# Mean over 8192 columns: the tail of the stream summed by VectorE alone, in seven pieces instead of five

## The chip, the cores and the metric

The kernel runs on one core of a Trainium2 chip. The metric is the device time of one execution, in microseconds (us), as the median of several runs. Six engines and queues appear in the text by their short names: DVE is VectorE, ACT is ScalarE, POOL is GpSimd, SP is SyncE, which here only issues DMAs, and the DMA queue behind SP is served by 16 DMA engines.

## What is computed

```python
x: (64, 256, 8192) float32
out = np.mean(x, axis=2)      # (64, 256)
```

That is 16384 rows of 8192 numbers, 536.87 MB to read, and one mean for each row, 64 KB to write.

## The kernel before

**Layout.** The 16384 rows are spread over 128 partitions, so a partition owns 128 rows. The rows are cut into three zones of 95, 17 and 16 rows a partition; within a zone a partition's rows lie one behind the other in memory. A load takes a pair of rows for each partition: 128 partitions by 16384 columns, 8 MB. Three buffers `buf0` to `buf2` take the pairs in turn.

**SP** issues every DMA, in program order. The first pair comes in three loads (lines 108, 109, 112), the next two at line 114, then a loop of 15 rounds with three loads each (line 121), then 15 loads written out (line 127). Each waits until DVE has freed its buffer (`free_sems`). The last pair of rows goes into `buf0`, called `tail` from there on, and it is cut into five pieces (line 133): SP waits once, for `buf0` to be free, and issues all five. The first four pieces land in `tail`, the last in the first columns of a small tile `fin`. Each piece has a semaphore of its own (`chunk_sems`). Behind them SP waits for POOL (`pool_sem`, line 134) and stores the scaled results of the first two zones (line 136, two stores), then it waits for `late_sem` and stores those of the last zone, `ends` (line 140). Nothing on SP can pass what stands ahead of it.

**DVE** sums a pair with one `tensor_reduce` (line 168 in the loop, line 178 for the first two of the last three pairs). For the last full pair and for the tail it uses the helper `halves` (line 151): one instruction adds the first half of a row to the second half element by element and also sums the result into one number, so that n columns take n / 2 steps. The instruction comes with a second one that reads the accumulator (DVE_READ_ACCUMULATOR2_ANT in the profile).

**The tail before.** `U` is 32 columns. The cuts are at columns 0, 9120, 13600, 15136, 15872 and 16384, so the pieces have 9120, 4480, 1536, 736 and 512 columns. Columns 0 to 8191 are the pair's first row; DVE sums it (4096 column halves) once the first piece is there. The second row is shared: of every one of the first four pieces ACT takes the first `mine[c]` columns (928, 1600, 544 and 256, line 207, with a running sum into one number), DVE the rest of the pieces 1 to 3 (2880, 992 and 480 columns, that is halves of 1440, 496 and 240). Each such sum is put into one of the eight columns `part(n)` behind the last piece in `fin`; seven are used, and POOL has zeroed the eighth (line 88) to keep the number even. When the last piece, all four ACT sums (`part_a`) and the DVE sums and POOL's zero (`part_d`) are there, `halves(fin, ...)` sums the 512 columns and the eight partial sums together (260 column halves), scales by 1 / 8192 and writes the last column of `ends`.

**POOL** scales all other results by 1 / 8192 in four instructions (line 97) after DVE's sum of the pair's first row (`owned_sem` at 4): 94, 2 and 16 columns into `scaled`, 15 into `ends`. When all four are done, SP may go on to the stores.

Of the kernel before, what the change touches and what calls it, by code (L numbers as in the profile page):

```python
# [5 lines left out]
F32 = mybir.dt.float32  # L6
ADD = mybir.AluOpType.add
X = mybir.AxisListType.X
COPY = mybir.ActivationFunctionType.Copy


def bass_global_avg_pool_1d_kernel(
# [6 lines left out]
    B, C, L = x.shape  # L19
# [20 lines left out]


    U = L // 256
    cuts = [0, L + 29 * U, L + 169 * U, L + 217 * U, L + 240 * U, 2 * L]
    mine = [29 * U, 50 * U, 17 * U, 8 * U]
    LAST = cuts[5] - cuts[4]
    NPART = 8

    flat = x.rearrange("b c l -> (b c) l")
    out_flat = out.rearrange("b c -> (b c)")
# [9 lines left out]
    with ExitStack() as ctx:  # L59
        sb = lambda n, s: ctx.enter_context(nc.sbuf_tensor(n, s, F32))  # L60
        sem = lambda n: ctx.enter_context(nc.semaphore(n))
        res = sb("res", [P, OWN - 1])
        scaled = sb("scaled", [P, EARLY])
        ends = sb("ends", [P, LATE])
        fin = sb("fin", [P, LAST + NPART])
        sb("pad", [P, (-nc.sbuf_base % ALIGN) // 4])
# [3 lines left out]
        free_sems = [sem(f"free_sem{i}") for i in range(NBUF)]  # L70
        first_sem = sem("first_sem")
        mixed_sem = sem("mixed_sem")
        chunk_sems = [sem(f"chunk_sem{c}") for c in range(5)]
        owned_sem = sem("owned_sem")
        part_d = sem("part_d")
        part_a = sem("part_a")
        pool_sem = sem("pool_sem")
        late_sem = sem("late_sem")
        out_sem = sem("out_sem")
# [2 lines left out]
        tail = bufs[0]  # L82
        part = lambda n: fin[:, LAST + n : LAST + n + 1]

        eng = nc.gpsimd
        eng.memset(part(NPART - 1), 0.0).then_inc(part_d, 1)  # L88
        eng.wait_ge(free_sems[0], LOADS0 + 1)
# [12 lines left out]
        eng = nc.sync  # L102
        def rows_of(n, k):
            z = 2 if n >= FROM[2] else 1 if n >= FROM[1] else 0
            return zone[z][:, (n - FROM[z]) * L : (n - FROM[z] + k) * L]

        a, z = rows_of(ZONE[0] - 1, 1), rows_of(ZONE[0], 1)
# [19 lines left out]
            eng.dma_start(bufs[b][:], rows_of(first_row(g), 2)).then_inc(in_sems[b], 16)  # L127
        eng.wait_ge(free_sems[0], LOADS0 + 1)
        two = rows_of(2 * NB, 2)
        for c in range(5):  # L130
            a, z = cuts[c], cuts[c + 1]
            dst = tail[:, a:z] if c < 4 else fin[:, 0:LAST]
            eng.dma_start(dst, two[:, a:z]).then_inc(chunk_sems[c], 16)  # L133
        eng.wait_ge(pool_sem, 4)
        for z in range(2):
# [11 lines left out]
        eng = nc.vector  # L147

        def halves(ap, to, done, scale=1.0):
            n = ap.shape[1] // 2  # L150
            eng.tensor_tensor_reduce(  # L151
                ap[:, 0:n],
                ap[:, 0:n],
                ap[:, n : 2 * n],
                scale=scale,
                scalar=0.0,
                op0=ADD,
                op1=ADD,
                accum_out=to,
            ).then_inc(done, 1)  # L160
# [29 lines left out]
                    )  # L190
        eng.wait_ge(chunk_sems[0], 16)
        halves(tail[:, 0:L], res[:, 2 * NB : 2 * NB + 1], owned_sem)
        for c in range(1, 4):
            eng.wait_ge(chunk_sems[c], 16)
            halves(tail[:, cuts[c] + mine[c] : cuts[c + 1]], part(3 + c), part_d)
        eng.wait_ge(chunk_sems[4], 16)
        eng.wait_ge(part_a, 4)
        eng.wait_ge(part_d, 4)
        halves(fin, ends[:, LATE - 1 : LATE], late_sem, inv)


        eng = nc.scalar
        for c in range(4):
            eng.wait_ge(chunk_sems[c], 16)
            a = cuts[c] if c else L
            ap = tail[:, a : a + mine[c]]
            eng.activation(ap, ap, COPY, accum_out=part(c)).then_inc(part_a, 1)  # L207


# [26 lines left out]
```

## Time and profile before

| | us |
|---|---|
| median of 3 runs | 1243.16 (1243.15 to 1243.31) |
| the profiled execution | 1243.06 |
| its span, first to last instruction | 1241.7 |
| HBM read 536.87 MB over the span | 432 GB/s |
| ACT: its four sums in the tail | 3.6 busy |
| POOL: its four scalings | 2.4 and 0.3 busy |

The profile comes from one execution. An "idle" time in brackets stands ahead of the instruction that it delayed, with what ended it. "SPq" is SP's queue, and its time is that of issuing DMAs, not of their transfers; the time of a transfer runs from its issue to its landing, so it includes the wait behind earlier transfers of the queue. In the row of a group, the numbers behind the first bar are the total busy time in us and the mean of one instruction in ns. A DVE group called CUSTOM_DVE_ANT_0 at line 151 is the helper `halves`; its column count is half of the columns that it sums. Among the landing times of the tail's five loads, the medians from issue are 32.2, 37.1, 38.5, 39.0 and 39.2 us: they stand behind the pair before them.

### The profile page before, as it was taken

What the parts mean: (1) busy time and instruction counts of PE and PEld (TensorE: products, weight loads), DVE (VectorE), ACT (ScalarE), POOL (GpSimd) and SP (SyncE); (2) the same over time, 40 slices, a digit from 0 to 9 for tenths busy, and PEclk for the clock granted to TensorE, in tenths of its full rate; (3) what the DMA queues carried; (4) which work ended last, traced back from release to release, by engine and by line L of the source; (5) the groups of instructions that cost most, each with busy time, mean ns of one, the idle gap of its engine ahead of it and who ended that gap; (6) DMA issues with size and microseconds to landing.
All of it is one profiled execution on the core that took longest, in us unless ns stands there. A gap on an engine that the chain in (4) does not pass through costs nothing. (4 is left out here: it accounts for less than half of the span.)

```text
span 1241.7 us, 549 instructions
## 1 busy us (share of the span) xinstructions
DVE 1084.1 (87%) x76; ACT 5.2 (0%) x9; POOL 2.9 (0%) x9
## 2 busy tenths in 40 slices
DVE  2898988989889898898898988989889898898987
ACT  0000000000000000000000000000000000000001
POOL 0000000000000000000000000000000000000000
DMA  9999999999999999999999999999999999999998
GB/s 405 439 439 439 439 435 410 439 439 439 439 439 433 412 439 439 439 439 439 426 418 439 439 439 439 439 422 422 439 439 439 439 439 422 422 439 439 439 439 374
DMA packets 10512, 536.94 MB, mean 432 GB/s; under 512 B 1552, under 2 KB 1552, under 8 KB 1936
## 3 DMA queue, kind: packets, MB, share of 16 engines
q1 hardware_dynamic: 10512, 536.94, 99.9%
HBM read 536.87 MB, written 0.07 MB: 432 GB/s over the span
## 5 line engine op out<-in xcount | busy, mean ns | idle before, releaser
L168 DVE TENSOR_REDUCE res<-buf 128x16384 f32 x60 | 1033.2, 17220 | 146.5 <-DVEq L167 146.5
L178 DVE TENSOR_REDUCE res<-buf 128x2 f32<-128x16384 f32 x2 | 34.4, 17220 | 4.0 <-DMA buf<-in_x_dram 4.0
L151 DVE CUSTOM_DVE_ANT_0 buf<-buf 128x4096 f32<-128x4096 f32 (+3 forms) x6 | 16.0, 2672 | 5.4 <-DMA buf<-in_x_dram 5.4
L207 ACT ACTIVATE buf<-buf 128x928 f32<-128x928 f32 (+3 forms) x4 | 3.6, 897 | 1233.7 <-DMA buf<-in_x_dram 1233.7
L97 POOL TENSOR_SCALAR scaled<-res 128x94 f32<-128x94 f32 (+2 forms) x3 | 2.4, 784 | 1235.0 <-DVE res L151 1234.8
L207 ACT ACT_TABLE_LOAD x1 | 1.3, 1283 | 0.7 <-PEq L221 0.7
L207 ACT ACTIVATION_READ_ACCUMULATOR buf<-buf 128x1 f32 x4 | 0.7, 187 | 0.0
L151 DVE CUSTOM_DVE_ANT_0 fin<-fin 128x260 f32<-128x260 f32 x1 | 0.4, 429 | 0.3 <-DMA fin<-in_x_dram 0.3
L97 POOL TENSOR_SCALAR ends<-res 128x15 f32<-128x15 f32 x1 | 0.3, 264 | 0.1
L151 DVE DVE_READ_ACCUMULATOR2_ANT res<- 128x1 f32 x3 | 0.3, 84 | 0.0
L151 DVE DVE_READ_ACCUMULATOR2_ANT fin<- 128x1 f32 x3 | 0.2, 81 | 0.0
L221 POOL MEMSET const-bfloat16-1.0<- 128x1 bf16 x1 | 0.1, 102 | 0.0
L221 POOL MEMSET const-uint8-127<- 128x1 uint8 x1 | 0.1, 102 | 0.0
L88 POOL MEMSET fin<- 128x1 f32 x1 | 0.1, 99 | 0.3 <-POOLq L221 0.3
L221 POOL MEMSET const-float32-0.0<- 128x1 f32 x1 | 0.1, 99 | 0.2 <-issue 0.2
L221 POOL MEMSET const-float32-1.0<- 128x1 f32 x1 | 0.1, 99 | 0.0
L151 DVE DVE_READ_ACCUMULATOR2_ANT ends<- 128x1 f32 x1 | 0.1, 82 | 0.0
## 6 DMA issues: line engine op xcount, KB each, us to landing
buf<-in_x_dram SPq DMA_DIRECT2D x1, 4560.0 KB, 32.2
buf<-in_x_dram SPq DMA_DIRECT2D x1, 4096.0 KB, 20.6
buf<-in_x_dram SPq DMA_DIRECT2D x1, 3072.0 KB, 11.4
buf<-in_x_dram SPq DMA_DIRECT2D x1, 2240.0 KB, 37.1
buf<-in_x_dram SPq DMA_DIRECT2D x1, 1024.0 KB, 4.6
buf<-in_x_dram SPq DMA_DIRECT2D x62, 40.3
buf<-in_x_dram SPq DMA_DIRECT2D x1, 768.0 KB, 38.5
buf<-in_x_dram SPq DMA_DIRECT2D x1, 368.0 KB, 39.0
```

Source lines behind the costliest of these rows:

```text
L88: eng.memset(part(NPART - 1), 0.0).then_inc(part_d, 1)
L97: eng.tensor_scalar(dst, src, inv, None, op0=mybir.AluOpType.mult).then_inc(pool_sem, 1)
L151: eng.tensor_tensor_reduce(ap[:, 0:n], ap[:, 0:n], ap[:, n : 2 * n], scale=scale, scalar=0.0, op0=ADD, op1=ADD, accum_out=to,).then_inc(do ...
L168: eng.tensor_reduce(sums[:, bass.ds(i, 1), b, :], bufs[b][:].rearrange("p (j l) -> p j l", j=2), X, ADD,).then_inc(free_sems[b], 1)
L178: eng.tensor_reduce(res[:, 2 * g : 2 * g + 2], bufs[b][:].rearrange("p (j l) -> p j l", j=2), X, ADD,).then_inc(free_sems[0] if b == 0 els ...
L207: eng.activation(ap, ap, COPY, accum_out=part(c)).then_inc(part_a, 1)
L221: nc = _bacc.Bacc("TRN2", target_bir_lowering=False, num_devices=1)
```

## The change

The tail is cut at columns 0, 8192, 9984, 12928, 14432, 15296, 15872 and 16384: seven pieces of 8192, 1792, 2944, 1504, 864, 576 and 512 columns. The first piece is now exactly the pair's first row. DVE sums every piece of the second row whole, as halves of 896, 1472, 752, 432 and 288 columns, into five partial sums; POOL's zero is the sixth, and the last sum takes 512 + 6 columns (259 column halves). The ACT program, its semaphore and its wait are gone. The last piece is the same 512 columns as before. In the changed kernel all lines from 11 on move up by one, and those behind the tail's loop by some more.

```diff
-COPY = mybir.ActivationFunctionType.Copy
...
     U = L // 256
-    cuts = [0, L + 29 * U, L + 169 * U, L + 217 * U, L + 240 * U, 2 * L]
-    mine = [29 * U, 50 * U, 17 * U, 8 * U]
-    LAST = cuts[5] - cuts[4]
-    NPART = 8
+    cuts = [0, L] + [L + n * U for n in (56, 148, 195, 222, 240)] + [2 * L]
+    PIECES = len(cuts) - 1
+    LAST = cuts[-1] - cuts[-2]
+    NPART = PIECES - 1
+    assert NPART % 2 == 0
...
-        chunk_sems = [sem(f"chunk_sem{c}") for c in range(5)]
+        chunk_sems = [sem(f"chunk_sem{c}") for c in range(PIECES)]
...
-        part_a = sem("part_a")
...
-        for c in range(5):
+        for c in range(PIECES):
             a, z = cuts[c], cuts[c + 1]
-            dst = tail[:, a:z] if c < 4 else fin[:, 0:LAST]
+            dst = tail[:, a:z] if c < PIECES - 1 else fin[:, 0:LAST]
...
-        for c in range(1, 4):
+        for c in range(1, PIECES - 1):
             eng.wait_ge(chunk_sems[c], 16)
-            halves(tail[:, cuts[c] + mine[c] : cuts[c + 1]], part(3 + c), part_d)
-        eng.wait_ge(chunk_sems[4], 16)
-        eng.wait_ge(part_a, 4)
-        eng.wait_ge(part_d, 4)
+            halves(tail[:, cuts[c] : cuts[c + 1]], part(c - 1), part_d)
+        eng.wait_ge(chunk_sems[PIECES - 1], 16)
+        eng.wait_ge(part_d, NPART)
         halves(fin, ends[:, LATE - 1 : LATE], late_sem, inv)
-
-
-        eng = nc.scalar
-        for c in range(4):
-            eng.wait_ge(chunk_sems[c], 16)
-            a = cuts[c] if c else L
-            ap = tail[:, a : a + mine[c]]
-            eng.activation(ap, ap, COPY, accum_out=part(c)).then_inc(part_a, 1)
```

## The prediction

> **What bounds the kernel now.** I read the page first, for which resource is full; then the chain that ended last; then the order of time of the last 60 us, because the diff touches nothing before it; then the shapes of the groups; then the loads and stores of the last stage.
>
> ```profile
> span 1241.7 us, 549 instructions
> DVE 1084.1 (87%) x76; ACT 5.2 (0%) x9; POOL 2.9 (0%) x9
> DMA  9999999999999999999999999999999999999998
> q1 hardware_dynamic: 10512, 536.94, 99.9%
> DMA 6%; DVE 3%; SPq 0%; issue 0%; DVEq 0%
> ```
>
> The one queue is full in every slice but the last: 536.94 MB take 99.9% of the time of sixteen engines, while VectorE (DVE) is busy for 87%. The kernel is a stream of loads, and everything else is wanted only to keep up. So a change in the tail can matter in two ways: by making the stream's last byte land at another time, or by making what follows that byte longer. The chain, in order of time, says the same of the end:
>
> ```profile
> 1200.62 39.18 DMA fin<-in_x_dram
> 1239.80 0.02 issue
> 1239.83 0.43 DVE fin L151
> 1240.26 0.01 DVE ends L151
> ```
>
> The last piece, issued at 1200.62, lands at 1239.80; VectorE starts on it 0.03 us later, works 0.43 us, and what is left up to 1241.7 is the store of the result. No ScalarE (ACT) instruction and no GpSimd (POOL) instruction is in this chain. The tail itself, in order of time:
>
> ```profile
> 1200.96 17.22 DVE L178 TENSOR_REDUCE res<-buf 128x2 f32<-128x16384 f32 x1 [2.16 <-DMA buf<-in_x_dram]
> 1220.27 4.42 DVE L151 CUSTOM_DVE_ANT_0 buf<-buf 128x4096 f32<-128x4096 f32 x1 [2.09 <-DMA buf<-in_x_dram]
> 1224.62 4.42 DVE L151 CUSTOM_DVE_ANT_0 buf<-buf 128x4096 f32<-128x4096 f32 x1
> 1228.96 0.08 DVE L151 DVE_READ_ACCUMULATOR2_ANT res<- 128x1 f32 x1
> 1231.01 4.43 DVE L151 CUSTOM_DVE_ANT_0 buf<-buf 128x4096 f32<-128x4096 f32 x1 [1.97 <-DMA buf<-in_x_dram]
> 1235.36 0.08 DVE L151 DVE_READ_ACCUMULATOR2_ANT res<- 128x1 f32 x1
> 1235.62 2.51 POOL L97 TENSOR_SCALAR scaled<-res 128x94 f32<-128x94 f32 x3 [1234.80 <-DVE res L151]
> 1236.35 1.66 DVE L151 CUSTOM_DVE_ANT_0 buf<-buf 128x1440 f32<-128x1440 f32 x1 [0.91 <-DMA buf<-in_x_dram]
> 1238.21 0.26 POOL L97 TENSOR_SCALAR ends<-res 128x15 f32<-128x15 f32 x1
> 1238.24 0.69 DVE L151 CUSTOM_DVE_ANT_0 buf<-buf 128x496 f32<-128x496 f32 x1 [0.22 <-DMA buf<-in_x_dram]
> 1238.50 0.82 SPq L136 DMA_DIRECT2D out_dram<-scaled  x2
> 1239.14 0.41 DVE L151 CUSTOM_DVE_ANT_0 buf<-buf 128x240 f32<-128x240 f32 x1 [0.20 <-DMA buf<-in_x_dram]
> 1239.47 0.19 ACT L207 ACTIVATION_READ_ACCUMULATOR buf<-buf 128x1 f32 x1
> 1239.48 0.08 DVE L151 DVE_READ_ACCUMULATOR2_ANT fin<- 128x1 f32 x1
> 1239.83 0.43 DVE L151 CUSTOM_DVE_ANT_0 fin<-fin 128x260 f32<-128x260 f32 x1 [0.26 <-DMA fin<-in_x_dram]
> 1240.29 0.33 SPq L140 DMA_DIRECT2D out_dram<-ends  x1
> ```
>
> The brackets carry the argument: ahead of every piece VectorE sat idle until a DMA landed, 1.97, 0.91, 0.22, 0.20 and 0.26 us. Its starts are therefore the landing times of the pieces (plus some 0.02 us each, which cancels in differences). ACT's last result is done at 1239.47 + 0.19 = 1239.66, that is 0.14 us before the last piece lands, so dropping ACT uncovers nothing by itself.
>
> **The change part by part.**
>
> *The two added loads.* The last pair still is 16384 columns in the same queue, and its last piece still is the same 512 columns; seven loads bring them where five did. From the starts above: 9120 columns took 1231.01 - 1220.27 = 10.74 us, or 1.1776 ns a column (the pair ahead took 19.31 for 16384, 1.179). At 1.1776 the smaller pieces should take 5.28, 1.81, 0.87 and 0.60; they took 5.34, 1.89, 0.90 and 0.69. So a piece costs 0.06, 0.08, 0.03 and 0.09 us beyond its bytes, 0.066 in the mean. Two more pieces: **+0.13 us**, with 0.06 and 0.18 as ends from the cheapest and the dearest of the four. The least is nothing; a gain is excluded, as the bytes and the queue stay the same. The upper end, far off, is a whole landing per load; that is a rival below. I take 0.13, for the added pieces (576 to 2944 columns) are of the sizes of those rows.
>
> *Where the pieces land.* With 1.1776 ns a column and 0.066 us a piece after the first, counted from 1220.27: 8192 columns at 1229.92, 1792 at 1232.09, 2944 at 1235.63, 1504 at 1237.46, 864 at 1238.55, 576 at 1239.29, 512 at 1239.96 (before: 1239.83).
>
> *What VectorE now does alone.* These groups give its price by columns:
>
> ```profile
> L151 DVE CUSTOM_DVE_ANT_0 buf<-buf 128x4096 f32<-128x4096 f32 x3 | 13.2, 4424 | 4.1 <-DMA buf<-in_x_dram 4.1
> L151 DVE CUSTOM_DVE_ANT_0 buf<-buf 128x1440 f32<-128x1440 f32 x1 | 1.7, 1659 | 0.9 <-DMA buf<-in_x_dram 0.9
> L151 DVE CUSTOM_DVE_ANT_0 buf<-buf 128x240 f32<-128x240 f32 x1 | 0.4, 409 | 0.2 <-DMA buf<-in_x_dram 0.2
> L151 DVE CUSTOM_DVE_ANT_0 fin<-fin 128x260 f32<-128x260 f32 x1 | 0.4, 429 | 0.3 <-DMA fin<-in_x_dram 0.3
> L97 POOL TENSOR_SCALAR scaled<-res 128x16 f32<-128x16 f32 x1 | 1.7, 1672 | 0.1
> L97 POOL TENSOR_SCALAR ends<-res 128x15 f32<-128x15 f32 x1 | 0.3, 264 | 0.1
> ```
>
> From 1440 to 4096 columns a half costs (4424 - 1659) / 2656 = 1.041 ns a column, and 1659 - 1440 x 1.041 = 160 ns stands fixed (240 columns by it: 410, measured 409). The halves of the new pieces are 4096, 896, 1472, 752, 432, 288 and, at the end, 259 columns: 4.42, 1.09, 1.69, 0.94, 0.61, 0.46 and 0.43 us. Back to back, the next starts 4.35 after a 4.42 (1220.27 to 1224.62). So: 4096 from 1229.92; 896 from 1234.27 to 1235.36, late by 2.18 but with nothing behind it yet; 1472 at its landing, 1235.63 to 1237.32; 752 from 1237.46 to 1238.40; 432 from 1238.55 to 1239.16; 288 from 1239.29 to 1239.75; the last at its landing, 1239.96. VectorE takes over 2.03 us (4.79 for the five middle pieces against 1.66 + 0.69 + 0.41 = 2.76) and hides them in its waits: ahead of the last five pieces it is still idle 0.27, 0.14, 0.15, 0.13 and 0.21. Cost on the path: **0**. If that cover were gone, what comes late is the 288 column piece, and only what exceeds 0.21 us reaches the end. The last half is one column shorter: 1 ns.
>
> *ScalarE leaves.*
>
> ```profile
> 0.72 1.28 ACT L207 ACT_TABLE_LOAD   x1 [0.72 <-PEq L221]
> 0.73 0.39 SPq L108 DMA_DIRECT2D buf<-in_x_dram  x1
> 1198.83 1.75 SPq L133 DMA_DIRECT2D buf<-in_x_dram  x4
> ```
>
> Its 5.2 us are off the chain, and the last sum's wait for it was over at 1239.66; 0. With it goes a table load of 1.28 us at the start, at 0.72, while SyncE's first load issues at 0.73 without waiting for it; 0.
>
> *GpSimd and SyncE.* The first row of the pair (8192 columns now, 9120 before) is done at 1234.34, not 1235.44, so GpSimd's scaling starts some 1.1 us earlier (0.18 after: 1234.52). SyncE issues the two stores of `scaled` when GpSimd is through, and the store of `ends` stands behind them in its order. GpSimd is sensitive to VectorE here: the 16 column scaling took 1672 ns beside the 264 of the 15 column one, and it ended at 1235.62 + 2.51 = 1238.13, just 0.12 after the 1440 column sum beside it ended (1236.35 + 1.66 = 1238.01). Now VectorE is never idle for long, so I let each of the four scalings get through in one gap: after 1235.36, 1237.32, 1238.40 and 1239.16, the last at 1239.28. The stores are issued 0.03 later, 1239.31 to 1240.13, and `ends` is wanted at 1239.96 + 0.46 = 1240.42. Margin 0.29; **0** on the path.
>
> The two added issues on SyncE go out with the others, 0.44 us each (1.75 / 4), so all seven from 1198.83 to 1201.9, the last 38 us before it lands: 0. Should the stores be issued early and cut in between the loads, they would cost little. In these stretches (busy columns, clock, share of the DMA engines, GB/s) the loads' landing at 1239.80 is followed by the two stores' packets, 0.44 of 0.2 us:
>
> ```profile
> 1239.60:1239.80 0.20, 0.00 (x0) 0.05 (x1) 0.00 (x0) 1.00 0.07 8
> 1239.80:1240.00 0.20, 0.17 (x1) 0.00 (x0) 0.00 (x0) 1.00 0.44 42
> out_dram<-scaled SPq DMA_DIRECT2D x1, 47.5 KB, 1.6
> out_dram<-ends SPq DMA_DIRECT2D x1, 8.0 KB, 1.4
> ```
>
> That is 0.09 us of the engines, and here they waited behind the loads.
>
> **The sum.** +0.13 + 0 + 0 + 0. The profiled execution took 1243.06 (span 1241.7 and 1.36 around it) and so gives 1243.19. The median of the runs, 1243.16, lies 0.10 above that execution, so for a median I write **1243.3**: +0.01%.
>
> **The rivals.**
>
> *GpSimd misses gaps.* If a scaling does not get through in a gap of 0.13 to 0.15 us, the last waits for the 288 column sum (1239.75 + 0.12 = 1239.87): the stores go out 1239.90 to 1240.72, and `ends` follows 0.30 late. If two gaps are missed, it waits for the very last sum (1240.39 + 0.12): stores from 1240.54 to 1241.36, 0.94 late. 1243.6 or 1244.2. For it: the 1672 ns row, and gaps smaller than the 264 ns that a free scaling takes. Against: the blocked scaling ended 0.12 after VectorE did, in a gap of 0.22. The Trainium skill, SBUF — State Buffer, section "Who interferes with whom", states that a VectorE instruction with two SBUF inputs and a GpSimd instruction that reads SBUF share a port, and that the one issued second is blocked for the whole of the other; by that rule a scaling that starts in a gap would in turn hold the next sum by up to its 264 ns, 0.05 beyond the last margin of 0.21, and give 1243.35. The trace agrees for the blocked scaling, but the 496 column sum, started 0.03 after a scaling, took 0.69 where 160 + 496 x 1.041 gives 0.68, so it shows no such hold.
>
> *Each added load pays a landing (the other side).* The shortest time from issue to landing in this trace is the 1.4 us of `ends`. If the stream could not overlap small loads, two more would cost 2 x 1.4 = 2.8 us: 1246.0, +0.23%. It decides from the point where a piece's bytes take less time than its landing, about 1.4 / 1.1776 = 1190 columns, and the 864, 576 and 512 column pieces are below that. Against it stand pieces of 736 and 512 columns that followed each other by 0.90 and 0.69 us, half of that. The Trainium skill, DMA: Bandwidth & Descriptors, section "Rules for kernel authors", asks for 1 MiB per DMA or more for full bandwidth, and "Anatomy of one DMA" puts the fixed part at some 2.0 us on GpSimd's path; an estimate by that page, unhidden, would be 4 us and 1247.3. The loads here come from SyncE, and the 0.69 us spacing speaks against any of it being paid in sequence.
>
> *ScalarE's absence shortens start or end.* At most the 1.28 us of its table load: 1242.0. Against: SyncE's first load at 0.73 did not wait for it.
>
> *The change moves nothing at all.* The loads set the end, and the cuts cost nothing: 1243.2. It lies within the forecast's own range.
>
> **How the numbers follow.** A measurement of this kernel can tell about 0.2% (2.5 us) from no change. Forecast, cuts at 0 to 0.18 us, 1243.1 to 1243.5: 0.76. GpSimd late: 0.16. ScalarE's share: 0.05. A landing per load: 0.03. The range takes in the first two up to 1244.2 and a tenth either way, and goes down by the spread of the runs (0.16, 1243.15 to 1243.31) below their lowest: 1242.9 to 1244.3; what it leaves out is under 0.1. Only a landing per load is over 0.2% away: slower 0.03; nothing I found reaches 2.5 us of gain: faster 0.01; the rest, 0.96, within.
>
> **What would show it.** Right: the last piece lands within 0.2 us of 1239.93, VectorE idle ahead of each of the last five pieces with the DMA as releaser, no ACT instruction, and the chain still ending DMA, last sum, store. The scalings on GpSimd stretched, but SyncE's two stores issued before 1240.1. Wrong: the stores of `scaled` ending after the last sum (first rival); pieces more than 1 us apart where the columns say 0.7 (second); a span unlike before with the same landing (third); or a last sum released by VectorE itself, which would mean that my prices for the halves are too low.

## The result, and the profile after

The changed kernel takes 1246.11 us in the median (1245.96 to 1246.63, 11 runs), the kernel before 1243.16 (1243.11 to 1243.32, 11 runs): the ratio is 1.0024, with a 95% interval of 1.0016 to 1.0032. The change is slower by 2.95 us. That lies outside the range on record, which ended at 1244.3. It happens to be the 1246.0 of the rival in which each added load pays a landing; the experiments show that this is a coincidence.

The page of the changed kernel, with the lines that answer to those shown of before:

```profile
span 1244.6 us, 546 instructions
DVE 1086.0 (87%) x80; POOL 4.9 (0%) x9
q1 hardware_dynamic: 10800, 536.94, 99.8%
DMA 6%; DVE 3%; SPq 0%; issue 0%; DVEq 0%
L167 DVE TENSOR_REDUCE res<-buf 128x16384 f32 x60 | 1033.2, 17220 | 149.0 <-DVEq L166 149.0
```

The queue is as full as before (99.8% against 99.9%), the chain has the same make-up, and VectorE's 60 sums of pairs take the same 17220 ns each. Only the idle time ahead of them has grown. The kernel before has the same row with less of it:

```profile
L168 DVE TENSOR_REDUCE res<-buf 128x16384 f32 x60 | 1033.2, 17220 | 146.5 <-DVEq L167 146.5
```

VectorE waited 149.0 - 146.5 = 2.5 us longer for loads, and it did so in the main loop, which the diff does not mention. The first wait, before anything has landed, makes up 0.2 of it. The order of time shows how it adds up. VectorE's first sum, some in the middle, and those ahead of the tail, in the changed kernel:

```profile
22.71 17.22 DVE L167 TENSOR_REDUCE res<-buf 128x16384 f32 x1 [22.71 <-DVEq L166]
584.14 17.22 DVE L167 TENSOR_REDUCE res<-buf 128x16384 f32 x1 [2.15 <-DVEq L166]
603.50 17.22 DVE L167 TENSOR_REDUCE res<-buf 128x16384 f32 x1 [2.14 <-DVEq L166]
622.85 17.22 DVE L167 TENSOR_REDUCE res<-buf 128x16384 f32 x1 [2.14 <-DVEq L166]
642.21 17.22 DVE L167 TENSOR_REDUCE res<-buf 128x16384 f32 x1 [2.14 <-DVEq L166]
1203.43 17.22 DVE L177 TENSOR_REDUCE res<-buf 128x2 f32<-128x16384 f32 x1 [2.13 <-DMA buf<-in_x_dram]
```

And in the kernel before:

```profile
22.49 17.22 DVE L168 TENSOR_REDUCE res<-buf 128x16384 f32 x1 [22.49 <-DVEq L167]
582.96 17.22 DVE L168 TENSOR_REDUCE res<-buf 128x16384 f32 x1 [2.15 <-DVEq L167]
602.27 17.22 DVE L168 TENSOR_REDUCE res<-buf 128x16384 f32 x1 [2.09 <-DVEq L167]
621.55 17.22 DVE L168 TENSOR_REDUCE res<-buf 128x16384 f32 x1 [2.06 <-DVEq L167]
640.86 17.22 DVE L168 TENSOR_REDUCE res<-buf 128x16384 f32 x1 [2.09 <-DVEq L167]
```

Between the first and the last of the 62 sums lie 61 intervals: (1203.43 - 22.71) / 61 = 19.356 us after, (1200.96 - 22.49) / 61 = 19.319 before. Every pair takes 0.037 us more, 2.3 us in all, and it does so evenly: 19.36, 19.35, 19.36 after, where before the intervals go up and down (19.31, 19.28, 19.31). So something that holds for the whole stream has changed.

The diff does change one such thing. `NPART` went from 8 to 6, so `fin` is 518 columns wide instead of 520, and `fin` stands ahead of the three buffers. A filler tile, `pad`, is meant to bring the buffers to a multiple of 4096 bytes in each partition, but its size is worked out from the end of `fin`, while tiles are placed at multiples of 32 bytes. In the built programs `fin` starts at byte 17536. Before it ends at 19616, a multiple of 32; 864 bytes of filler end at 20480 = 5 x 4096. After it ends at 19608; the filler gets 872 bytes for that, is placed at 19616 and ends at 20488, and the buffers start at **20512**, 32 bytes past the multiple.

The tail of the changed kernel, in order of time:

```profile
1222.80 4.43 DVE L150 CUSTOM_DVE_ANT_0 buf<-buf 128x4096 f32<-128x4096 f32 x1 [2.15 <-DMA buf<-in_x_dram]
1232.52 4.42 DVE L150 CUSTOM_DVE_ANT_0 buf<-buf 128x4096 f32<-128x4096 f32 x1 [0.94 <-DMA buf<-in_x_dram]
1237.13 4.02 POOL L96 TENSOR_SCALAR scaled<-res 128x94 f32<-128x94 f32 x3 [1236.31 <-DVE res L150]
1238.27 1.69 DVE L150 CUSTOM_DVE_ANT_0 buf<-buf 128x1472 f32<-128x1472 f32 x1 [0.30 <-DMA buf<-in_x_dram]
1240.09 0.94 DVE L150 CUSTOM_DVE_ANT_0 buf<-buf 128x752 f32<-128x752 f32 x1
1241.21 0.61 DVE L150 CUSTOM_DVE_ANT_0 buf<-buf 128x432 f32<-128x432 f32 x1 [0.17 <-DMA buf<-in_x_dram]
1241.23 0.72 POOL L96 TENSOR_SCALAR ends<-res 128x15 f32<-128x15 f32 x1
1241.97 0.82 SPq L135 DMA_DIRECT2D out_dram<-scaled  x2
1241.98 0.46 DVE L150 CUSTOM_DVE_ANT_0 buf<-buf 128x288 f32<-128x288 f32 x1
1242.61 0.43 DVE L150 CUSTOM_DVE_ANT_0 fin<-fin 128x259 f32<-128x259 f32 x1 [0.17 <-DMA fin<-in_x_dram]
1243.07 0.33 SPq L139 DMA_DIRECT2D out_dram<-ends  x1
```

From the last full pair's arrival to the last sum it takes 1242.61 - 1222.80 = 19.81 us where it took 1239.83 - 1220.27 = 19.56. The last sum is still released by the DMA of `fin`, and the chain still ends with load, sum, store. The 0.25 us more are taken apart below.

### The profile page after: what moved, and what is told of

The parts are those of the page before. It is cut to its first block, busy times and chain, and to the rows that moved or that the text cites. A ratio compares the mean times of both kernels' runs of the same rounds, so it can differ in the third digit from the quotient of the medians.

```text
span 1244.6 us, 546 instructions
## 1 busy us (share of the span) xinstructions
DVE 1086.0 (87%) x80; POOL 4.9 (0%) x9
## 3 DMA queue, kind: packets, MB, share of 16 engines
q1 hardware_dynamic: 10800, 536.94, 99.8%
## 5 line engine op out<-in xcount | busy, mean ns | idle before, releaser
L167 DVE TENSOR_REDUCE res<-buf 128x16384 f32 x60 | 1033.2, 17220 | 149.0 <-DVEq L166 149.0
L177 DVE TENSOR_REDUCE res<-buf 128x2 f32<-128x16384 f32 x2 | 34.4, 17220 | 4.1 <-DMA buf<-in_x_dram 4.1
L150 DVE CUSTOM_DVE_ANT_0 buf<-buf 128x4096 f32<-128x4096 f32 (+5 forms) x8 | 17.9, 2257 | 3.8 <-DMA buf<-in_x_dram 3.6
```

Source lines behind the costliest of these rows:

```text
L150: eng.tensor_tensor_reduce(ap[:, 0:n], ap[:, 0:n], ap[:, n : 2 * n], scale=scale, scalar=0.0, op0=ADD, op1=ADD, accum_out=to,).then_inc(do ...
L167: eng.tensor_reduce(sums[:, bass.ds(i, 1), b, :], bufs[b][:].rearrange("p (j l) -> p j l", j=2), X, ADD,).then_inc(free_sems[b], 1)
L177: eng.tensor_reduce(res[:, 2 * g : 2 * g + 2], bufs[b][:].rearrange("p (j l) -> p j l", j=2), X, ADD,).then_inc(free_sems[0] if b == 0 els ...
```

## The experiments: which part of the change costs what

**Theory A**: the buffers' address, through the width of `fin`, slows every load. **Theory B**: the missing ScalarE program does. **Theory C**: other differences of the program, the number of semaphores or the piece sizes, do.

**The changed kernel with the address put back.**

```diff
-        sb("pad", [P, (-nc.sbuf_base % ALIGN) // 4])
+        sb("pad", [P, (-nc.sbuf_base % ALIGN) // 32 * 8])
```

> The changed kernel with only the filler tile ahead of the buffers 8 bytes a partition shorter, so that the three buffers start on a multiple of 4096 bytes again, as they do in the kernel before (they start 32 bytes past one in the changed kernel). Theory A, the buffers' address slows every load: the pair interval goes back from 19.36 to 19.33 us, the last full pair is taken up near 1220.3 instead of 1222.8, and the time is 1243.3 to 1243.5 (before plus the two added pieces). Theory B, the missing ScalarE program slows the stream: no change, 1246.1. Theory C, the program's other differences (more semaphores, other piece sizes): no change, 1246.1.

Measured: 1243.65 us (1243.24 to 1243.94, 10 runs), ratio to before 1.0003, interval 0.9993 to 1.0012. VectorE's first and last sum of a pair:

```profile
22.82 17.22 DVE L167 TENSOR_REDUCE res<-buf 128x16384 f32 x1 [22.82 <-DVEq L166]
1201.26 17.22 DVE L177 TENSOR_REDUCE res<-buf 128x2 f32<-128x16384 f32 x1 [2.15 <-DMA buf<-in_x_dram]
```

The pairs are back at (1201.26 - 22.82) / 61 = 19.319 us. A filler of 864 bytes instead of 872 takes away 2.46 of the 2.95 us. The time is still 0.15 us above the 1243.5 at which theory A's range ended; that rest is the subject of a later experiment. Theories B and C fall for that part, as ScalarE is still missing here and the pieces and semaphores are those of the changed kernel.

**The kernel before with the address moved**, nothing else changed. The theories A1, A2 and A3 in the expectations are ways in which the loss could go with the offset. The edit for 32 bytes is this; for 64, 128, 224 and 256 bytes it adds 16, 32, 56 and 64 columns.

```diff
-        sb("pad", [P, (-nc.sbuf_base % ALIGN) // 4])
+        sb("pad", [P, (-nc.sbuf_base % ALIGN) // 4 + 8])
```

> The kernel before with only the filler tile 32 bytes a partition longer, so that the buffers start 32 bytes past a multiple of 4096, as in the changed kernel; ScalarE, cuts and semaphores as before. Theory A: 2.5 us more, 1245.7, the pair interval 19.36. Theories B and C: no change, 1243.2, the pair interval 19.33.

> The kernel before with the buffers 256 bytes past a multiple of 4096. Theory A with a loss per misaligned 256-byte write: no change, 1243.2. Theory A with a loss per 4096-byte boundary (or another unit over 256 bytes): about as slow as at 32 bytes, 1245.7. Theories B and C: 1243.2.

> The kernel before with the buffers 128 bytes past a multiple of 4096. The 32 byte shift cost 2.66 us and the 256 byte shift nothing. Theory A1, a fixed loss for each row that does not start on a 256 byte boundary (one write more per row): 1245.9, as at 32. Theory A2, a loss that grows with the offset inside the 256 bytes (4 times that at 32): 1253.8. Theory A3, only the offset inside 64 or 128 bytes counts: 1243.2.

> The kernel before with the buffers 224 bytes past a multiple of 4096. Theory A1, fixed loss per row: 1245.9. Theory A2, growing with the offset (7 times that at 32): 1261.8. Theory A2 the other way, growing with what is left to the next boundary (32 bytes here, 224 there): a seventh, 1243.6. Theory A3: 1245.9.

> The kernel before with the buffers 64 bytes past a multiple of 4096. 32 and 224 bytes cost 2.66 and 2.60 us, 128 bytes 2.01. A fixed loss per row with less at offsets of 128: 1245.9. Less for offsets that are multiples of 64: 1245.2.

| buffers start at a multiple of 4096 plus | median us (10 runs each) | ratio to before, interval | us a pair |
|---|---|---|---|
| 0 (the kernel before, run beside them) | 1243.19 to 1243.21 | | 19.319 |
| 32 | 1245.87 | 1.0021, 1.0011 to 1.0031 | 19.356 |
| 64 | 1245.23 | 1.0017, 1.0007 to 1.0026 | 19.349 |
| 128 | 1245.22 | 1.0016, 1.0006 to 1.0026 | 19.348 |
| 224 | 1245.81 | 1.0021, 1.0011 to 1.0030 | 19.356 |
| 256 | 1243.19 | 1.0000, 0.9990 to 1.0009 | 19.316 |

With 32 bytes, the same two sums of the kernel before stand here:

```profile
22.89 17.22 DVE L168 TENSOR_REDUCE res<-buf 128x16384 f32 x1 [22.89 <-DVEq L167]
1203.63 17.22 DVE L178 TENSOR_REDUCE res<-buf 128x2 f32<-128x16384 f32 x1 [2.15 <-DMA buf<-in_x_dram]
```

The 32 byte offset alone makes the kernel before nearly as slow as the changed one (1245.87 against 1246.11), with the same 19.356 us a pair, so theory A is shown from both sides. 256 bytes cost nothing, so 256 is enough here and the 4096 in the code asks for more than these runs show to matter. Inside the 256 bytes the loss is nearly the same at 32 and at 224: a fixed loss (A1) comes closest, though 64 and 128 bytes cost a quarter less (2.0 against 2.6 us). The 64 byte run came out as expected if offsets that are multiples of 64 cost less, but that describes the numbers and gives no cause. A loss that grows with the offset (A2) falls, either way round, and so does A3, by which 128 bytes would have cost nothing. The Trainium skill, DMA: Bandwidth & Descriptors, section "How a descriptor splits into AXI transactions", gives a rule of this kind: transactions of 256 bytes that must start at a multiple of 256, one more for a long run that does not, with the unused bytes still paid for. The boundary agrees, and one more transaction at each offset would fit the like loss at 32 and 224; that the price would follow the unused bytes does not agree, as there are 32 of them in the one case and 224 in the other. The page's example is a read, and these are writes into SBUF.

**VectorE alone, with the five pieces of before and the address kept.** The ScalarE program goes; the first piece's 928 columns of the second row become a sum of their own, the others are summed whole.

```diff
-        halves(fin, ends[:, LATE - 1 : LATE], late_sem, inv)
+        halves(fin[:, 0 : LAST + 4], ends[:, LATE - 1 : LATE], late_sem, inv)
...
+        halves(tail[:, L : cuts[1]], part(0), part_d)
         for c in range(1, 4):
             eng.wait_ge(chunk_sems[c], 16)
-            halves(tail[:, cuts[c] + mine[c] : cuts[c + 1]], part(3 + c), part_d)
+            halves(tail[:, cuts[c] : cuts[c + 1]], part(c), part_d)
```

> The kernel before without ScalarE's program: VectorE sums the same five pieces alone (the first piece's 928 columns of the second row as a sum of their own, the others whole), and the last sum takes 516 columns; the tile stays 520 wide, so the buffers keep their address. Theory A: 1243.2, as VectorE's longer sums (464, 2240, 768, 368 column halves, some 4.6 us) are partly hidden; the 2240 column half from 1236.35 ends at 1238.84, the 768 one at 1239.80, the 368 one at 1240.34, so the last sum starts about 0.5 late: 1243.7. Theory B: 1245.7 or more. Theory C: 1243.2 to 1243.7.

Measured: 1244.30 us (1244.18 to 1244.83), ratio 1.0009, interval 0.9999 to 1.0018. The pairs keep their 19.317 us, so B is out here too. It is 0.6 above the expectation of theory A, 1243.7. Its tail in order of time:

```profile
1239.90 0.54 DVE L147 CUSTOM_DVE_ANT_0 buf<-buf 128x368 f32<-128x368 f32 x1
1240.18 0.39 POOL L93 TENSOR_SCALAR ends<-res 128x15 f32<-128x15 f32 x1
1240.59 0.82 SPq L132 DMA_DIRECT2D out_dram<-scaled  x2
1240.60 0.43 DVE L147 CUSTOM_DVE_ANT_0 fin<-fin 128x258 f32<-128x258 f32 x1
1241.46 0.43 SPq L136 DMA_DIRECT2D out_dram<-ends  x1
```

VectorE is the bound: the last sum has no releaser in brackets and starts at 1240.60. And the first rival of the prediction happens here: GpSimd is through only at 1240.57, SyncE issues the two stores of `scaled` until 1241.41, and the store of `ends` goes out at 1241.46, 0.43 after the last sum ended at 1241.03, where it was 0.03 in the kernel before (1240.29 after 1240.26). That was left out of the expectation.

**The rest: late stores or added loads.** With the address put back the changed kernel is still 0.44 us above the 1243.21 of before. Its stores (KB each, us from issue to landing) and the end of its SyncE queue:

```profile
out_dram<-scaled SPq DMA_DIRECT2D x1, 8.5 KB, 2.1
out_dram<-ends SPq DMA_DIRECT2D x1, 8.0 KB, 1.9
```

```profile
1220.56 4.43 DVE L150 CUSTOM_DVE_ANT_0 buf<-buf 128x4096 f32<-128x4096 f32 x1 [2.08 <-DMA buf<-in_x_dram]
1239.51 0.82 SPq L135 DMA_DIRECT2D out_dram<-scaled  x2
1240.16 0.43 DVE L150 CUSTOM_DVE_ANT_0 fin<-fin 128x259 f32<-128x259 f32 x1 [0.23 <-DMA fin<-in_x_dram]
1240.62 0.33 SPq L139 DMA_DIRECT2D out_dram<-ends  x1
```

From the last full pair's arrival to the last sum it takes 1240.16 - 1220.56 = 19.60 us, 0.04 more than the 19.56 of before. But the last store takes 1.9 us instead of 1.4, and the two stores ahead of it are issued at 1239.51, not 1238.50. This execution is the slowest of the ten (1243.94), so its 1.9 us need not be those of the median. So I let GpSimd scale the first two zones' results early, which do not depend on the tail, and SyncE store them then; once on this kernel and once on the kernel before.

```diff
-        eng.wait_ge(owned_sem, 4)
         for dst, src in [
...
         ]:
+            if dst.shape[1] == LATE - 1:
+                eng.wait_ge(owned_sem, 4)
...
-        eng.wait_ge(pool_sem, 4)
+        eng.wait_ge(pool_sem, 3)
...
+        eng.wait_ge(pool_sem, 4)
         eng.wait_ge(late_sem, 1)
```

> The changed kernel with the buffers back on a multiple of 4096, and GpSimd's three scalings into the two first zones' results no longer behind the sum of the pair's first row: only the fourth waits for it, and SyncE issues the two stores as soon as the three are done. Theory D, the 0.44 us that the aligned kernel still is slower come from the stores being issued late (1239.51) so that the last store takes 1.9 us instead of 1.4: 1243.2 to 1243.3. Theory E, they come from the two added loads: no change, 1243.65. If early stores cut in between the loads: up to 0.3 us more.

> The kernel before with the same early scaling and early stores. Theory D: no change or a little faster, 1243.1 to 1243.2, as the last store already takes only 1.4 us. Theory E: no change, 1243.2. If early stores cut in between the loads: up to 0.3 us more.

Measured: 1243.32 us (1243.19 to 1243.39) and 1243.24 (1243.15 to 1243.72), ratios 1.0001 and 1.0001, intervals 0.9991 to 1.0010 for both. In the first the last store is at its 1.4 us again:

```profile
out_dram<-ends SPq DMA_DIRECT2D x1, 8.0 KB, 1.4
```

Its runs lie within 0.20 us, those of the aligned kernel without the early scaling within 0.70, and eight of those ten are slower than the slowest here. So scaling and storing early takes away 0.33 of the 0.44 us while both added loads stay: theory E can't account for all of it, and theory D fits. The early stores did not cut in between the loads: they landed 37.8 and 38.0 us after their issue, behind them. Two reservations stay. The medians differ by less than the intervals of the ratios can tell, and how the late stores charge is not shown: in the kernel before moved by 128 bytes the two stores were issued 1.2 us ahead of the last (1241.25 and 1242.46), and it took 1.4 us; in the five-piece kernel above they were issued 0.9 us ahead, and it took 1.5. So the time between the issues does not set the price by itself. No version was faster than the kernel before beyond the noise.

**Does every misaligned pair pay?** A gap ahead of one buffer or of two moves only these by 32 bytes. This is the edit for two; for the third buffer alone the gap stands ahead of that one, and for the first alone the filler is 32 bytes longer and a gap of 224 bytes behind `buf0` brings the others to a multiple of 256 again.

```diff
-        bufs = [sb(f"buf{i}", [P, 2 * L]) for i in range(NBUF)]
+        bufs = [sb("buf0", [P, 2 * L])]
+        sb("gap", [P, 8])
+        bufs += [sb(f"buf{i}", [P, 2 * L]) for i in range(1, NBUF)]
```

> The kernel before with a gap ahead of the third buffer alone, so that only it starts 32 bytes past a multiple of 4096; the other two keep their address. Theory A: a third of the pairs are slow, so a third of the 2.66 us of all three: 0.9, 1244.1. If one misaligned buffer already slows the whole stream: 1245.9. If the loss came from where the tile sizes put things otherwise: 1243.2.

> The kernel before with a gap behind the first buffer, so that the second and third start 32 bytes past a multiple of 256 and the first on one. Three such buffers cost 2.66 us, one cost 0.09 instead of the third that was expected. Theory F, two paces meet: the loads as such come at 19.32 us a pair in the mean (19.27 to 19.39 when all buffers are aligned), a misaligned pair can be written no faster than in 19.36, and an aligned one in 19.27 or less, so that the stream runs at the slower of 19.32 and the mean of the written pairs: (2 x 19.36 + 19.27) / 3 = 19.33, some 0.5 to 1 us more, 1243.7 to 1244.2. Theory G, only the first buffer's address matters: 1243.2. Theory H, any second misaligned buffer makes the whole stream slow: 1245.9.

> The kernel before with the first buffer alone 32 bytes past a multiple of 256, and the other two on one (256 bytes further on than before). Theory F: as with the third buffer alone, (19.36 + 2 x 19.27) / 3 = 19.30 is below 19.32, so 0 to 0.1 us more, 1243.2 to 1243.3. Theory G: all of the loss, 1245.9.

Measured: the third buffer alone 1243.28 us (ratio 1.0001, 0.9991 to 1.0010), the first alone 1243.30 (1.0001, 0.9991 to 1.0010), two buffers 1244.30 (1.0009, 0.9999 to 1.0019). The expectation of a third for one buffer was wrong: one costs 0.09 or 0.15 us, two cost 1.15 and all three 2.66. Theories G and H fall. VectorE's starts with two buffers moved show why a sum of losses is the wrong picture:

```profile
564.07 17.22 DVE L170 TENSOR_REDUCE res<-buf 128x16384 f32 x1 [2.13 <-DVEq L169]
583.44 17.22 DVE L170 TENSOR_REDUCE res<-buf 128x16384 f32 x1 [2.15 <-DVEq L169]
602.73 17.22 DVE L170 TENSOR_REDUCE res<-buf 128x16384 f32 x1 [2.07 <-DVEq L169]
622.09 17.22 DVE L170 TENSOR_REDUCE res<-buf 128x16384 f32 x1 [2.15 <-DVEq L169]
641.44 17.22 DVE L170 TENSOR_REDUCE res<-buf 128x16384 f32 x1 [2.13 <-DVEq L169]
660.75 17.22 DVE L170 TENSOR_REDUCE res<-buf 128x16384 f32 x1 [2.09 <-DVEq L169]
```

The intervals are 19.37, 19.29, 19.36, 19.35, 19.31: the short one comes back every third pair, when the aligned buffer is filled, and it is shorter than the 19.319 that all pairs take in the mean when all are aligned. That fits theory F, two paces in a row: the loads come at 19.32 us a pair in the mean, a misaligned pair can be written no faster than in 19.36, an aligned one in about 19.30, and the stream runs at the slower of the two means. The 19.30 is read from these rows (on record the theory had 19.27 or less), so what it gives for two buffers is no test of it. One misaligned pair in three gives (19.36 + 2 x 19.30) / 3 = 19.32, hidden; two give 19.34, three 19.36. The measured means are 19.322, 19.336 and 19.356. The runs with one moved buffer agree: in the main loop the pairs that go into it take 19.349 us in the mean (the third) or 19.347 (the first), the pairs into the other two 19.307 to 19.317, so the loss is there each time and the next two pairs make up for most of it. The writing pace itself is not in any view, so F is a reading that fits, not shown. What in the DMA engines makes it, and why 64 and 128 bytes cost less, stays open; the alignment on the HBM side wasn't tried.

## Why the prediction was wrong

**The step that failed** stands in its first paragraph: I read only the last 60 us "because the diff touches nothing before it", and priced the loads with "the bytes and the queue stay the same". The diff touches `NPART`, `NPART` sets the width of `fin`, and the tile stands ahead of the buffers. The bytes and the queue are the same, the place where they are written is not, by 32 bytes. That term, 0.037 us for each of 61 pairs, was left out of the sum; it measured 2.46 us of the 2.95 when it was taken out of the changed kernel (1246.11 - 1243.65), and 2.66 when it was put into the kernel before.

**The added loads**: forecast +0.13, from 0.06 to 0.18. With early scaling in both kernels, seven pieces take 1243.32 us and five 1243.24: 0.08 more, within the spread of the runs. From the last full pair's arrival to the last sum, the traces with the address put back show less than the forecast: 19.60 us, and 19.58 with early scaling (1240.07 - 1220.49), against 19.56 before. With all buffers 32 bytes off, seven pieces take 19.81 us and five 19.67 (1242.65 - 1222.98 in the kernel before so moved), 0.14 more. So the term is small, as forecast, but 0.02 to 0.04 us when the buffers are aligned. One difference beside the number of pieces was not tested alone: of the pieces that land in `buf0` behind the first, all three start 128 bytes past a multiple of 256 in the kernel before, and only one of five does in the aligned kernel with seven.

**VectorE's sums**: forecast 1.09, 1.69, 0.94, 0.61, 0.46 and 0.43 us, hidden. The groups of the changed kernel by shape:

```profile
L150 DVE CUSTOM_DVE_ANT_0 buf<-buf 128x1472 f32<-128x1472 f32 x1 | 1.7, 1693 | 0.3 <-DMA buf<-in_x_dram 0.3
L150 DVE CUSTOM_DVE_ANT_0 buf<-buf 128x896 f32<-128x896 f32 x1 | 1.1, 1084 | 0.0
L150 DVE CUSTOM_DVE_ANT_0 buf<-buf 128x752 f32<-128x752 f32 x1 | 0.9, 942 | 0.1
L96 POOL TENSOR_SCALAR scaled<-res 128x94 f32<-128x94 f32 x1 | 1.1, 1142 | 1236.3 <-DVE res L150 1236.3
L96 POOL TENSOR_SCALAR scaled<-res 128x2 f32<-128x2 f32 x1 | 1.7, 1694 | 0.1
L96 POOL TENSOR_SCALAR scaled<-res 128x16 f32<-128x16 f32 x1 | 1.0, 1026 | 0.1
L96 POOL TENSOR_SCALAR ends<-res 128x15 f32<-128x15 f32 x1 | 0.7, 716 | 0.1
```

The three rows, 1084, 1693 and 942 ns, are within 10 ns of the forecast, and the sums are hidden: the last sum waits 0.17 us for the DMA, forecast 0.21.

**GpSimd**: forecast was one scaling in each gap. That is what the last four rows are: the 2 column one takes as long as the 1472 column sum beside it, the others end with the next sums. The stores were issued from 1241.97 to 1242.79, and `ends` was wanted at 1243.04: margin 0.25, forecast 0.29. But I took the margin on the issue for the whole price. The two stores were issued 1.1 us ahead of that of `ends` instead of 1.8, and it took 1.5 us from issue to landing in this profile and 1.9 in that of the aligned kernel, against 1.4 before. Scaling and storing early took 0.33 us off the median of the aligned kernel, where I had 0. So the late stores have a price although SyncE was free again in time for `ends`; why they have it stays open.

The traces also answer the other half of the first rival, that a scaling begun first would hold VectorE's next sum. In the kernel before and in seven of those with moved buffers, the last scaling starts 0.03 to 0.07 us ahead of the 496 column sum and takes its free 0.26 to 0.27 us, and the sum takes 0.67 to 0.69, as in the kernel before with early scaling, where no scaling is near (0.67). With 128 bytes the sum starts 0.01 us first, and the scaling takes 0.78. VectorE held GpSimd here; GpSimd did not hold VectorE.

**ScalarE's absence**: forecast 0. With ScalarE gone and the address in place the pairs keep their 19.32 us (19.319 with seven pieces, 19.317 with five), and VectorE's first sum starts no earlier (22.82 us with seven pieces, 22.49 in the kernel before), so 0 is right.

**A landing per added load**: 1246.0 was written for it, and the time came out at 1246.11. It is refuted all the same: the last pieces of the changed kernel follow each other by 1241.98 - 1241.21 = 0.77 and 1242.61 - 1241.98 = 0.63 us, well below the 1.4 us of a landing, and with the address put back all seven pieces stay while 2.46 us go. A time that fits is not a mechanism that is shown.

## What to carry to other kernels

Ask of a change what it moves in memory, not only what it does in time: the width of a small tile decides where the large ones behind it start, and in a stream that is 99.9% full a small loss in each load adds up: here 0.037 us a pair, 61 times over. Round a filler from the place where the next tile will really be put, and look at the buffers' addresses in the built program, of both kernels, before costing anything. When two profiles differ by a small time, compare the interval of the main loop first; those 61 intervals made 2.3 of the 2.95 us plain to see, and none of that was in the tail.

## What the runs showed of the hardware

Loads of 64 KB rows into SBUF made this kernel 0.16 to 0.21% longer when all three buffers started 32, 64, 128 or 224 bytes past a multiple of 256, and next to nothing longer when one of three did so by 32 bytes (0.09 and 0.15 us). In the aligned kernel with early scaling SyncE's second store was held at its issue, with the last full pair, the seven pieces and the first store still under way:

```profile
1202.74 22.06 SPq L136 DMA_DIRECT2D out_dram<-scaled  x1
```

It cost nothing there, since SyncE had nothing else to do until 1240.58; in the kernel before with early scaling, where five pieces were under way, the two stores took 0.90 us to issue. Where between the two the limit lies was not measured, and no run had a load standing behind a store held so.
